# Output projection as seven block products in float16 parts, and a first value projection in plain float32

## The chip, the cores and the metric

The kernel runs on one core of a Trainium2 chip. Its time is the device time of that core in microseconds (us). The engines are named as in the profile: PE is TensorE with its matmuls, PEld its weight loads, DVE is VectorE, ACT is ScalarE, POOL is GpSimd, and SP is the engine whose queue issues nearly all DMAs. The program fixes the order of the instructions on each engine's queue.

## The reference, cut to what matters

One layer over 4096 frames of width 1024, all in float32:

```python
u = rms_norm(h, norm_g)                      # 4096 x 1024
p = u @ w_in                                 # 1024 x 4616: q, k, v, z of eight heads,
(sb_q, sb_k, sb_v, sb_z,                     #   q, k, v, o, z of four heads, two gates
 m_q, m_k, m_v, m_o, m_z, m_i, m_f) = split(p)
sb = stick_breaking_attention(sb_q, sb_k, sb_v) * silu(sb_z)
ml = head_layer_norm(mlstm_chunkwise(conv(m_q, m_k), m_v, m_i, m_f) * sigmoid(m_o)) * silu(m_z)
mix = concatenate([sb, ml])                  # 4096 x 1024
h = h + mix @ w_out                          # the output projection, 1024 x 1024
out = rms_norm(h, final_norm_g)
```

## The kernel before, in words

A frame tile is 128 frames; there are 32. A block is four tiles. The program makes four sweeps over the eight blocks: two for the stick-breaking heads (four heads each), two for the mLSTM heads (two heads each), and then the output projection, called stage C here. Normalised frames are transposed once, cut into a high and a low float16 part (`U`), stored to DRAM (`scr_u`, `u_store` L469) and read again by each sweep. Weights are scaled by a power found from their largest element (`Prep.top` L269, `Prep.scale` L282) and cut into float16 parts in the same way (`Prep.split` L293). A product of two cut operands takes three matmuls, high by high, high by low and low by high.

The order of the work is written out by hand. Time is counted in quanta: one quantum is the 24 matmuls of one weight group against one block (`t_quantum` L473), or the same amount of other matmuls. Helper steps are hung on a quantum with `at(g, phase, fn)` and issued by `run(g, phase)` ahead of its matmuls ("pre"), after half of them ("mid") or after its finishing step ("post"). Since the queues are in order, a helper step that makes PE wait holds all matmuls behind it.

**Start (L1180 to L1281).** SP loads frame tiles 0 and 1, the first value weights with the gate columns (four pieces of 256 KB and one of 32 KB), tiles 2 and 3, and the weight groups q0, k0; q1, k1, z0, z1 follow as buffers come free. Each weight group goes through `top` (DVE), a transpose on PE in `scale` (L284) with a short DVE chain after it, and `split` on POOL or DVE with ACT between. The value weights go through it first, and only then the value projections of tiles 0 to 2 run (`n_mm` L486, 264 columns, 24 float16 matmuls each; the fourth comes a little later through `sb_nat`). Then q1 and k1 are prepared, and the first quantum (q0) starts. In that quantum and the next, `z0.scale` and `z1.scale` are hung on "mid", between the two halves of the matmuls, and their `top` on "pre".

**Stage C (L1050 to L1178).** During the last block of the mLSTM the eight pieces of `w_out` are loaded and cut into two float32r parts (`wo_load` L1052, ACT and POOL). For each frame tile the mixed result is read from DRAM (`m_load` L1096), cut into two float32r parts (`m_split` L1110: ACT and DVE), and multiplied by the two halves of `w_out`: 24 matmuls of 512 columns for one half tile (`c_mm` L1119), accumulated in one PSUM bank. `c_add` (L1129) adds the residual on DVE and squares on ACT; `c_norm` (POOL) and `c_out` (DVE) normalise, and SP stores. The very last half tile is done in two pieces of 256 columns (`c_last` L1142). The last steps of the mLSTM's last block overlap the stage's first quanta.

The core of a product in stage C before:

```python
for k in range(KT):
    for j, (a, w) in enumerate(((0, wh), (1, wh), (0, wl))):
        PE.matmul(ps, u[:, a, k, :], w[:, cs], start=..., stop=...)
```

The functions that the change touches:

Of the kernel before, what the change touches and what calls it, by code (L numbers as in the profile page):

```python
# [9 lines left out]
F32 = mybir.dt.float32  # L10
# [10 lines left out]
DM = 1024  # L21
# [18 lines left out]
S_A = 2.0 ** 15  # L40


@with_exitstack
def hymba_kernel(ctx: ExitStack, tc: tile.TileContext, x, norm_g, w_in, b_ig, b_fg, conv_w,
# [9 lines left out]
    scr_m = dram.tile([NT, 128, KT, 128], F32, name="scr_m")  # L54
    scr_M = dram.tile([ML_H, SEQ], F32, name="scr_M")
# [6 lines left out]
              scr_u, scr_m, scr_M, scr_E, flag)  # L62
# [136 lines left out]
def main_pass(ctx, tc, x2, norm_g, win, win_k, b_ig, b_fg, conv_w, conv_b, hn_g, wout_k, fn_g,  # L199
              out2, scr_u, scr_m, scr_M, scr_E, flag):  # L200
# [6 lines left out]
    st = ctx.enter_context(tc.tile_pool(name="st", bufs=5))  # L207
# [27 lines left out]
    SX = const.tile([128, 2, 2, 3], F32, name="SX")  # L235
    idf = const.tile([128, 128], F32, name="idf")
# [10 lines left out]
    D1 = const.tile([128, 512], F32, name="D1")  # L247

# [271 lines left out]
    def sb_scales(s):  # L520

        for pair in range(2):
            q, k, z = (inv(WTS[s, f"{n}{pair}"]) for n in "qkz")
# [3 lines left out]
            V.tensor_scalar(out=SX[:, s, pair, 2:3], in0=z, scalar1=1.0 / (S_QKV * S_A), scalar2=inv(WNS[s]),  # L527
                            op0=ALU.mult, op1=ALU.mult)
# [416 lines left out]
    at(sb_g(NB) - 1, "post", lambda: sb_scales(1))  # L945
# [103 lines left out]
    WO = {}  # L1049
    gl = ml_g(2 * NB - 1)  # L1050

    def wo_load(i):  # L1052
        box = []

        def ld():
            r = stage()
            half, k0 = (1, 2 * i) if i < 4 else (0, 2 * i - 8)
            SP.dma_start(out=r.rearrange("p (k c) -> p k c", k=2), in_=wout_k[:, k0:k0 + 2, 512 * half:512 * half + 512])
            box.append(r)

        def sp():
            key = ("ba"[i // 4], i % 4)
            if i < 6:
                WO[key] = [wp.tile([128, DM], F32R, tag="wT", name="wT", bufs=T_SLOTS) for _ in range(2)]
            else:
                t = wp.tile([128, 2 * DM], F32R, tag="wna", name="wna", bufs=2)
                WO[key] = [t[:, 0:DM], t[:, DM:2 * DM]]
            split(*WO[key], box.pop(), G)
        return ld, sp

    for i in range(8):
        ld, sp = wo_load(i)
        gi = gl + (1 + i if i < 3 else 2 + i)
        at(gi, "pre", ld)
        at(gi + 1, "mid", sp)
    for i, gm in enumerate((gl + 2, gl + 3, c_g - 1, c_g)):
        at(gm, "pre", lambda i=i: m_load(i))
        at(gm + 2, "mid", lambda i=i: m_split(i))
# [39 lines left out]

    def c_mm(ps, i, half, c0, n, mid=None):  # L1119
        u = mb[i // 2][:, i % 2]  # L1120
        for k in range(KT):
            wh, wl = WO["ab"[half], k // 2]
            cs = slice((k % 2) * 512 + c0, (k % 2) * 512 + c0 + n)
            for j, (a, w) in enumerate(((0, wh), (1, wh), (0, wl))):
                PE.matmul(ps, u[:, a, k, :], w[:, cs], start=(k == 0 and j == 0), stop=(k == KT - 1 and j == 2))  # L1125
            if k == 3 and mid:
                mid()

    def c_add(ps, hsl, sq):  # L1129
        V.tensor_tensor(out=hsl, in0=ps, in1=hsl, op=ALU.add)  # L1130
        A.activation(out=ph_tile("kl0", list(hsl.shape)), in_=hsl, func=AF.Square, scale=DM ** -0.5, accum_out=sq)  # L1131
# [254 lines left out]
```

## Time and profile before

| | |
|---|---|
| median of three runs | 2305.04 us (2304.14 to 2309.72) |
| the profiled execution, its own time | 2303.64 us |
| span from its first to its last instruction | 2301.9 us |
| PE busy | 2211.8 us, 96% |
| DVE, ACT, POOL busy | 1319.9, 1007.7, 719.3 us |
| TensorE clock granted, mean | 0.986 of full speed |

The profiled execution lies 1.4 us under the median of the runs, and 1.7 us of its time lie outside the span. The page cuts the span into 40 slices of 57.5 us; a digit is the busy share in tenths:

```profile
PE   4699999999999999999999999999999999999998
DVE  6477777756666666755555555654544445433332
POOL 2277667754555556511111112200000013100000
PEclk7899999999999999999999999999999999999999
```

In the first two slices PE is busy for four and six tenths and its clock is granted only in part. From the third slice to the last PE is full, and stage C fills the last six.

### The profile page before, as it was taken

The numbers are of one execution on the slowest core, as the hardware profiler recorded it, in microseconds if no ns is written. First come the engines' busy times: TensorE is split into PE (matmuls) and PEld (weight loads), VectorE is DVE, ScalarE is ACT, GpSimd is POOL, SyncE is SP. The second block draws the span as 40 slices with busy tenths as digits, with TensorE's granted clock in tenths as the row PEclk, the third lists the DMA queues.
The fourth block names the chain that finished last, engine by engine and source line by source line (L and its number), as shares of the span: only waits on it lengthen the run. The fifth ranks groups of instructions, "written<-read, shape, count | busy, mean of one in ns | idle before, by whom it ended". The sixth has DMA issues, their size and how long they took to land.

```text
span 2301.9 us, 36279 instructions
## 1 busy us (share of the span) xinstructions
PE 2211.8 (96%) x13945; PEld 1526.6 (66%) x13945; DVE 1319.9 (57%) x2725; ACT 1007.7 (44%) x1806; POOL 719.3 (31%) x1134
## 2 busy tenths in 40 slices
PE   4699999999999999999999999999999999999998
PEld 3366566666666666567767665666667677888887
DVE  6477777756666666755555555654544445433332
ACT  3477667656666666533333333222333334222221
POOL 2277667754555556511111112200000013100000
PEclk7899999999999999999999999999999999999999
DMA  6244444411111122112222232221222224444442
GB/s 184 52 90 93 93 98 97 112 46 47 65 57 56 56 67 84 59 51 74 74 74 74 74 92 47 65 65 57 60 55 65 61 74 138 146 138 150 152 137 93
DMA packets 221917, 193.98 MB, mean 84 GB/s; under 512 B 108084, under 2 KB 177768, under 8 KB 221736
## 3 DMA queue, kind: packets, MB, share of 16 engines
q1 hardware_dynamic: 221720, 191.59, 29.4%
q8 instruction: 111, 1.82, 0.3%
q14 instruction: 70, 0.57, 0.1%
q10 hardware_dynamic: 16, 0.00, 0.0%
HBM read 141.09 MB, written 50.46 MB: 83 GB/s over the span
## 4 chain that ended last, share of the span: by engine, by line
PE 73%; DVE 6%; issue 1%; ACT 1%; DMA 0%; POOL 0%; POOLq 0%; DVEq 0%; ACTq 0%
PE ps_pj L480 31%; PE ps_pj L492 17%; PE ps_pj L1125 15%; PE ps_zu L823 1%; DVE z L778 1%; PE ps_at L617 1%; PE ps_o L633 1%; PE ps_zu L866 1%; PE ps_zu L867 1%; DVE c L738 1%; PE ps_at L824 1%; PE ps_o L848 1%; PE ps_zu L848 1%; PE ps_at L894 1%; PE ps_zu L586 1%
## 5 line engine op out<-in xcount | busy, mean ns | idle before, releaser
L480 PE MATMUL ps_pj<-U,wT 128*128 128x512 f16 x4608 | 1045.0, 382 | 0.0
L480 PEld LDWEIGHTS <-wT 128*128 128x128 f16 x4608 | 452.5, 99 | 494.4 <-issue 11.4
L492 PEld LDWEIGHTS <-U 128*128 128x128 f16 x4608 | 452.1, 98 | 82.8 <-DVE kl L565 11.9
L492 PE MATMUL ps_pj<-wna,U 128*128 128x256 f16 (+1 forms) x3072 | 361.7, 276 | 17.4 <-DVE kl L565 7.5
L1125 PE MATMUL ps_pj<-wT,U 128*128 128x512 f32 (+1 forms) x1164 | 267.8, 387 | 0.0
L1125 PEld LDWEIGHTS ps_pj<-wT,U 128*128 128x128 f32 x1164 | 216.6, 188 | 44.3
L601 POOL TENSOR_TENSOR sA<-sA,bP 128x510 f32<-128x510 f32 x128 | 151.7, 1185 | 199.2 <-DVE bP L600 180.4
L600 DVE TENSOR_TENSOR_SCAN bP<-bP,D 128x512 f32<-128x512 f32 x128 | 162.9, 1273 | 53.1 <-POOL bP L592 52.9
L492 PE MATMUL ps_pj<-wnb,U 128*128 128x256 f16 x1536 | 178.1, 273 | 0.0
L1131 ACT ACTIVATE kl<-st 128x512 f32<-128x512 f32 (+1 forms) x65 | 40.7, 625 | 274.1 <-DVE st L1130 265.8
L879 POOL TENSOR_SCALAR rs<-mv 128x4 f32<-128x4 f32 x32 | 8.0, 250 | 483.7 <-DVE kl L773 448.4
L774 ACT ACTIVATE kl<-ps_pj,SC 128x512 f32<-128x512 f32 x64 | 44.0, 687 | 242.0 <-PE ps_pj L480 208.9
L1130 DVE TENSOR_TENSOR st<-ps_pj,st 128x512 f32<-128x512 f32 (+1 forms) x65 | 44.4, 683 | 173.9 <-PE ps_pj L1125 170.7
L825 DVE TENSOR_TENSOR bP<-ps_zu,bP 128x512 f32<-128x512 f32 x32 | 22.1, 691 | 203.5 <-PE ps_at L824 202.4
L778 DVE SCALAR_TENSOR_TENSOR z<-kl,CT,z 128x512 f32<-128x512 f32 x144 | 118.3, 821 | 19.8 <-ACT z L775 15.2
L622 DVE SCALAR_TENSOR_TENSOR ATl<-ps_at,ATh 128x512 f16<-128x512 f32 (+1 forms) x128 | 87.8, 686 | 41.3 <-ACT ATh L621 39.2
L810 POOL TENSOR_SCALAR_AFFINE_SELECT bP<-bP 128x512 f32<-128x512 f32 x32 | 24.3, 760 | 270.0 <-DVE bP L809 239.8
L787 ACT ACTIVATE v<-ps_pj,SC 128x256 f32<-128x256 f32 x64 | 30.3, 474 | 168.8 <-PE ps_pj L492 168.2
L1170 POOL TENSOR_SCALAR ss<-hs 128x1 f32<-128x1 f32 x31 | 9.6, 311 | 292.3 <-ACT kl L1131 292.3
L563 ACT ACTIVATE kh<-ps_pj 64x512 f16<-64x512 f32 x128 | 75.6, 590 | 57.4 <-PE ps_pj L480 39.1
L1125 PE MATMUL ps_pj<-wna,U 128*128 128x512 f32 (+1 forms) x396 | 92.8, 383 | 0.0
L537 ACT ACTIVATE zml<-ps_pj,SC 128x512 f32<-128x512 f32 x32 | 22.0, 687 | 159.8 <-DMA scr_m<-zml 144.8
(233 smaller groups left out, 3458.8 us busy)
## 6 DMA issues: line engine op xcount, KB each, us to landing
U<-scr_u SPq DMA_DIRECT2D x96, 512.0 KB
st<-in_x_dram SPq DMA_DIRECT2D x40, 512.0 KB
scr_u<-U SPq DMA_DIRECT2D x32, 512.0 KB
out_dram<-st SPq DMA_DIRECT2D x31, 512.0 KB
st<-in_w_in_dram SPq DMA_DIRECT2D x28, 512.0 KB
z<-scr_m SPq DMA_DIRECT2D x56, 256.0 KB
st<-in_x_dram SPq DMA_DIRECT2D x96, 128.0 KB
scr_m<-z SPq DMA_DIRECT2D x32, 256.0 KB
```

The source lines that it names most:

```text
L480: PE.matmul(p3, wt[:, a, k, :], u[:, :, b, k, :], start=(k == 0 and i == 0), stop=(k == KT - 1 and i == 2))
L492: PE.matmul(ps[:, c0:c0 + n], u[:, a, k, :], w[:, b, k, 0:n], start=first and j == 0, stop=last and j == len(order) - 1)
L563: A.activation(out=kh[d, h, 128:640], in_=ps[e], func=AF.Copy, scale=S_QKV)
L600: V.tensor_tensor_scan(out=bf, data0=bf, data1=D1[:, ::-1], initial=1.0, op0=ALU.mult, op1=ALU.max)
L601: G.tensor_tensor(out=sg[:, :, 0:255], in0=sg[:, :, 0:255], in1=b[:, :, 1:256], op=ALU.mult)
L622: V.scalar_tensor_tensor(out=l[:, i:, :], in0=ps[:, i:, :], scalar=S_A, in1=h[:, i:, :], op0=ALU.mult, op1=ALU.subtract)
L774: A.activation(out=raw[:, 3:515], in_=ps, func=AF.Copy, scale=inv(sid))
L778: V.scalar_tensor_tensor(out=y, in0=raw[:, t:t + 512], scalar=CT[:, 8 * t + grp:8 * t + grp + 1], in1=y, op0=ALU.mult, op1=ALU.add)
L848: PE.matmul(ps[:, j, :], mK[hh][:, c, :], vaug(p0 + c, hh), start=True, stop=True)
L1125: PE.matmul(ps, u[:, a, k, :], w[:, cs], start=(k == 0 and j == 0), stop=(k == KT - 1 and j == 2))
L1130: V.tensor_tensor(out=hsl, in0=ps, in1=hsl, op=ALU.add)
L1131: A.activation(out=ph_tile("kl0", list(hsl.shape)), in_=hsl, func=AF.Square, scale=DM ** -0.5, accum_out=sq)
```

## The change

**Stage C.** Frame tiles are taken in pairs. The two tiles of a pair and the two halves of the 1024 inner columns make a 2 x 2 block matrix A (rows: tile 2p and 2p+1; columns: inner columns 0 to 511 and 512 to 1023); `w_out` makes a 2 x 2 block matrix B. A times B is formed by seven block products instead of eight, in Winograd's form of Strassen's scheme. With A and B scaled to a common largest value (`total_top`), the left operands are

```
o=0: a11   o=1: s1 = a21+a22   o=2: a12   o=3: s2 = s1-a11
o=4: s4 = a12-s2   o=5: s3 = a11-a21   o=6: a22
```

and the right ones are the like sums of B. Both sides are cut into float16 parts; a block product is 4 x 3 = 12 matmuls of 512 columns. Products 0, 3, 5, 6 accumulate in one PSUM bank, 1 and 4 in a second, 2 has a third. DVE reads a bank after each product and adds it, scaled back, to the residual (`c_add`), also between products that go on accumulating in it.

The right operands are built during the last mLSTM sweep (`wo_top`, `wo_build`): eight loads for the maxima, eight again for the sums, ACT scales, POOL forms the sums and the low parts, ACT the high parts; three of the seven go to DRAM (`scr_w`) and are read back when the buffers of the last block's weights come free (`tw_load`). The left operands of pair p are made by `m_load`, `m_top` (four DVE maxima), `m_bound` (a matmul against a tile of ones on PE, then a short DVE chain), `m_scale` (ACT), `m_combine` (four sums on POOL), `m_high` (ACT), `m_low` (three on DVE, four on POOL). They are hung on steps counted from the pair's first product t0:

```diff
-    def c_mm(ps, i, half, c0, n, mid=None):
-        u = mb[i // 2][:, i % 2]
-        for k in range(KT):
-            wh, wl = WO["ab"[half], k // 2]
...
+    def total_top(src, n, top, out_scale, out_back, back):
+        ps = ps_tile("zu", [128, 8])
+        PE.matmul(ps[:, 0:n], ones, src, start=True, stop=True)
+        mx = sm.tile([128, 1], F32, tag="wx", name="wx")
+        V.tensor_reduce(out=mx, in_=ps[:, 0:n], op=ALU.max, axis=AX.X)
+        V.tensor_scalar(out=mx, in0=mx, scalar1=1e-30, scalar2=1.0 / top, op0=ALU.max, op1=ALU.mult)
+        V.reciprocal(out=out_scale, in_=mx)
+        V.tensor_scalar(out=out_back, in0=mx, scalar1=back, scalar2=None, op0=ALU.mult)
...
+    def m_top(p):
+        un[p] = sm.tile([128, 6], F32, tag="mtop", name="mtop", bufs=4)
+        for i, t in enumerate(mt[p]):
+            V.tensor_reduce(out=un[p][:, i:i + 1], in_=t.rearrange("p k t -> p (k t)"), op=ALU.max, axis=AX.X,
+                            apply_absolute_value=True)
+
+    def m_bound(p):
+        u = un[p]
+        total_top(u[:, 0:4], 4, M_TOP, u[:, 4:5], u[:, 5:6], SO[:, 1:2])
+
+    def m_scale(p, js):
+        for j in js:
+            A.activation(out=mt[p][j], in_=mt[p][j], func=AF.Copy, scale=un[p][:, 4:5])
+
+    def m_combine(p):
+        a11, a12, a21, a22 = mt[p]
...
+        G.tensor_tensor(out=s1, in0=a21, in1=a22, op=ALU.add)
+        G.tensor_tensor(out=s2, in0=s1, in1=a11, op=ALU.subtract)
+        G.tensor_tensor(out=s4, in0=a12, in1=s2, op=ALU.subtract)
+        G.tensor_tensor(out=s3, in0=a11, in1=a21, op=ALU.subtract)
+        mt[p] = [a11, s1, a12, s2, s4, s3, a22]
...
+    def m_low(p, os):
+        for o in os:
+            (V if o in (0, 2, 6) else G).tensor_tensor(out=mo[p][:, o, 1], in0=mt[p][o], in1=mo[p][:, o, 0], op=ALU.subtract)
...
+    def c_product(p, o, ps, first, last):
+        a, (wh, wl) = mo[p][:, o], TW[o]
+        for k in range(4):
+            for i, (l, r) in enumerate(((0, wh), (1, wh), (0, wl))):
+                PE.matmul(ps, a[:, l, k, :], r[:, k, :], start=first and k == 0 and i == 0, stop=last and k == 3 and i == 2,
+                          skip_group_check=True)
+
+    def c_add(p, ps, i, half):
+        t = xt[2 * p + i][:, half * 512:(half + 1) * 512]
+        V.scalar_tensor_tensor(out=t, in0=ps, scalar=un[p][:, 5:6], in1=t, op0=ALU.mult, op1=ALU.add)
...
+    for p in range(NP):
+        seq += [(p, 0), (p - 1, 6)] if p else [(p, 0)]
+        seq += [(p, o) for o in ((1, 2, 3, 4, 5) if p < NP - 1 else (1, 3, 2, 5, 4, 6))]
...
+        atp(t0 - 13, lambda p=p: m_load(p))
+        atp(t0 - 9, lambda p=p: m_top(p))
+        atp(t0 - 8, lambda p=p: m_bound(p))
+        atp(t0 - 7, lambda p=p: m_scale(p, (2, 3)))
+        atp(t0 - 7, lambda p=p: m_scale(p, (0, 1)))
+        atp(t0 - 6, lambda p=p: m_combine(p))
+        atp(t0 - 5, lambda p=p: m_high(p, (0, 2, 6)))
+        atp(t0 - 4, lambda p=p: m_low(p, (0, 2, 6)))
+        atp(t0 - 4, lambda p=p: m_high(p, (1, 3)))
+        atp(t0 - 3, lambda p=p: m_low(p, (1, 3)))
+        atp(t0 - 3, lambda p=p: m_high(p, (4, 5)))
+        atp(t0 - 2, lambda p=p: m_low(p, (4, 5)))
```

Each step of `seq` is issued after what is hung on it. `c_norm` and `c_out` of a pair's first tile stand on the first two steps of the next pair, those of its second tile on the third and fourth. The last half tile is no longer cut in two.

**Start.** The value weights with the gates are loaded right behind frame tile 0 into one float32 tile `vraw`, multiplied by `norm_g` (first half DVE, second half POOL) and used as they are; the transposed frames are kept in float32 (`u32`) for this. `v_mm` makes one tile's value projection with eight float32 matmuls. The scale of the value weights is found later and only scales the result. The frames' float16 parts and their stores (`u_parts`) come after that, the preparation of q0 and k0 is moved ahead of them, q1 and k1 are prepared around the first quanta, and z0 and z1 later than before. The float16 parts of the value weights, which the next seven blocks need, are made on POOL and ACT in quanta 8 and 10.

```diff
+        def v_mm(p):
+            ps = vps[p] = ps_tile("pj", [128, 512])
+            for k in range(KT):
+                PE.matmul(ps[:, 0:264], u32[p][:, k, :], vraw[:, k, :], start=(k == 0), stop=(k == KT - 1))
...
-        u_first(0, lambda: u_scale(1))
-        pv.top()
-        pv.scale()
-        pv.split([G, V, G, V, V])
...
+        u_scale(1)
+        v_mm(0)
+        u_first(1)
+        v_top()
+        u_stats(2)
+        v_mm(1)
+        v_scale()
+        v_fin(0)
...
+        qk[0].split([G, V])
+        u_parts(0, V)
+        u_parts(1, V)
+        v_fin(2)
+        qk[1].top()
+        v_mm(3)
+        qk[1].scale()
+        qk[1].split([G, V])
+        u_parts(2, V)
+        v_fin(3)
+        u_parts(3, V)
...
+        qk[2].top()
+        at(2, "mid", qk[2].scale)
+        at(2, "mid", lambda: qk[2].split([G, V]))
+        at(2, "post", qk[3].top)
+        at(3, "mid", qk[3].scale)
...
+            at(3 + i, "post" if i == 0 else "pre", lambda box=box: box[0].top())
+            at(4 + i, "mid", lambda box=box: box[0].scale())
...
+        at(8, "mid", lambda: G.tensor_scalar(out=vs, in0=vs, scalar1=SC[:, WNS[0], 0:1], scalar2=None, op0=ALU.mult))
+        at(10, "pre", lambda: A.activation(out=pn[:, 0], in_=vraw, func=AF.Copy))
+        at(10, "post", lambda: G.tensor_tensor(out=pn[:, 1], in0=vraw, in1=pn[:, 0], op=ALU.subtract))
```

The pool of staging tiles grows from five to six.

## Rows read from the trace of the kernel before

**Rows 1.** Stretches: length, then busy time per engine, clock granted, DMA share, GB/s.
```profile
0.00:20.00 20.00, 8.02 (x40) 7.31 (x41) 10.29 (x27) 6.61 (x14) 6.26 (x16) 0.81 0.81 239
...
0.00:118.65 118.65, 71.95 (x359) 43.40 (x360) 65.19 (x161) 45.86 (x95) 34.75 (x52) 0.80 0.42 118
1938.40:2293.10 354.70, 354.70 (x1613) 294.86 (x1611) 138.85 (x239) 78.12 (x192) 35.09 (x69) 1.00 0.41 140
```

**Rows 2.** Timeline of PE in stage C: start, length, line, shape, count.
```profile
2260.00 8.32 PE L1125 MATMUL ps_pj<-wT,U 128*128 128x512 f32 x36
2268.16 2.88 PE L1125 MATMUL ps_pj<-wna,U 128*128 128x512 f32 x12
2270.88 8.32 PE L1125 MATMUL ps_pj<-wT,U 128*128 128x512 f32 x36
...
2290.07 1.60 PE L1125 MATMUL ps_pj<-wT,U 128*128 128x256 f32 x12
2291.51 1.60 PE L1125 MATMUL ps_pj<-wna,U 128*128 128x256 f32 x12
```

**Rows 3.** Timeline of PE in an mLSTM sweep: float16 quantum, then float32 matmuls.
```profile
1508.26 5.34 PE L480 MATMUL ps_pj<-U,wT 128*128 128x512 f16 x24
1513.44 0.61 PE L848 MATMUL ps_o<-v,ATh 128*128 128x130 f32 x4
1513.89 0.61 PE L848 MATMUL ps_zu<-v,ATh 128*128 128x130 f32 x4
```

**Rows 4.** Groups by line from 1900 us on: shapes, count, busy, mean ns, idle before.
```profile
L1130 DVE TENSOR_TENSOR st<-ps_pj,st 128x512 f32<-128x512 f32 x63 | 43.5, 691 | 171.1 <-PE ps_pj L1125 167.8 <-DMA st<-in_x_dram 3.3
L1131 ACT ACTIVATE kl<-st 128x512 f32<-128x512 f32 x63 | 39.8, 632 | 269.9 <-DVE st L1130 261.6 <-issue 8.2
L251 DVE TENSOR_TENSOR U<-z,U 128x512 fp32r<-128x512 f32 x56 | 36.2, 688 | 37.0 <-ACT U L250 37.0
L250 ACT ACTIVATE U<-z 128x512 fp32r<-128x512 f32 x56 | 31.9, 617 | 0.0
L1178 DVE SCALAR_TENSOR_TENSOR st<-st,ss,O 128x512 f32<-128x512 f32 x31 | 23.1, 746 | 0.0
...
L1171 POOL TENSOR_TENSOR ss<-ss,mhalf 128x1 f32<-128x1 f32 x31 | 17.7, 570 | 2.6
```

**Rows 5.** Timeline of DVE in the start: two maxima over 512 columns.
```profile
67.42 1.27 DVE L273 TENSOR_REDUCE wm<-ATh 128x4 f32<-128x512 f32 x2
```

**Rows 6.** Timeline of DVE and POOL: start, and first stick-breaking sweep.
```profile
16.13 1.54 POOL L301 TENSOR_TENSOR bP<-bP,wgs 128x512 f32<-128x512 f32 x1 [7.55 <-DVE wgs L291]
...
422.74 1.09 POOL L601 TENSOR_TENSOR sA<-sA,bP 128x510 f32<-128x510 f32 x1 [1.15 <-DVE bP L600]
...
423.94 2.13 POOL L378 TENSOR_TENSOR U<-st,U 128x1024 f16<-128x1024 f32 x1
...
427.49 1.27 POOL L691 TENSOR_TENSOR z<-z,O 128x512 f32<-128x512 f32 x1
...
431.05 1.20 DVE L378 TENSOR_TENSOR U<-st,U 128x1024 f16<-128x1024 f32 x1
431.27 1.92 POOL L601 TENSOR_TENSOR sA<-sA,bP 128x510 f32<-128x510 f32 x1 [1.69 <-DVE bP L600]
```

**Rows 7.** Timeline of PE in the start, with the idle time before and its releaser.
```profile
23.93 5.44 PE L492 MATMUL ps_pj<-wna,U 128*128 128x264 f16 x24 [7.16 <-ACT wna L296]
...
55.04 5.22 PE L480 MATMUL ps_pj<-U,wT 128*128 128x512 f16 x12
69.40 0.48 PE L284 MATMUL ps_zu<-idf,wmb 128*128 128x128 f32 x1 [9.13 <-DVE wmb L280]
...
84.91 0.48 PE L284 MATMUL ps_zu<-idf,wmb 128*128 128x128 f32 x1 [7.04 <-DVE wmb L280]
...
117.78 0.60 PE L617 MATMUL ps_at<-idf,sA 128*128 128x128 f32 x4
```

**Rows 8.** Timeline at the end: the last store's issue.
```profile
2296.08 0.90 SPq L1162 DMA_DIRECT2D out_dram<-st  x1
```

More of the change, by code (lines that the diff above doesn't have):

```diff
@@ L40 @@
 S_A = 2.0 ** 15
+M_TOP = 8192.0
 @with_exitstack
@@ L1056, in ld @@
             r = stage()
-            half, k0 = (1, 2 * i) if i < 4 else (0, 2 * i - 8)
-            SP.dma_start(out=r.rearrange("p (k c) -> p k c", k=2), in_=wout_k[:, k0:k0 + 2, 512 * half:512 * half + 512])
+            SP.dma_start(out=r, in_=wout_k[:, i, :])
             box.append(r)
[L1061 to L1064, printed above, removed]
-            else:
-                t = wp.tile([128, 2 * DM], F32R, tag="wna", name="wna", bufs=2)
-                WO[key] = [t[:, 0:DM], t[:, DM:2 * DM]]
-            split(*WO[key], box.pop(), G)
@@ L1080, in main_pass, with tw_load @@
+    for j in range(4):
+        wo_build(j, g3 + 20 + ML_SLOTS * j)
+    def tw_load(o):
+        t = [wp.tile([128, 4, 512], F16, tag="wT", name="wT", bufs=T_SLOTS) for _ in range(2)]
+        for i in range(2):
+            SP.dma_start(out=t[i], in_=scr_w[o - 4, :, i])
+        TW.append(t)
+    for o in (4, 5, 6):
+        at(gl + 2 * o - 5 if o < 6 else gl + 6, "pre", lambda o=o: tw_load(o))
     fng = [None, None]
@@ L1119, in c_mm @@
-    def c_mm(ps, i, half, c0, n, mid=None):
-        u = mb[i // 2][:, i % 2]
-        for k in range(KT):
-            wh, wl = WO["ab"[half], k // 2]
[L1123 to L1131, printed above, removed]
@@ new lines, in c_add, with c_square @@
+    def c_add(p, ps, i, half):
+        t = xt[2 * p + i][:, half * 512:(half + 1) * 512]
+        V.scalar_tensor_tensor(out=t, in0=ps, scalar=un[p][:, 5:6], in1=t, op0=ALU.mult, op1=ALU.add)
+    def c_square(p, i, half):
+        t = 2 * p + i
+        if t not in hs2:
+            hs2[t] = sm.tile([128, 2], F32, tag="hs2", name="hs2", bufs=4)
+        A.activation(out=ph_tile("kl0", [128, 512]), in_=xt[t][:, half * 512:(half + 1) * 512], func=AF.Square, scale=DM ** -0.5,
+                     accum_out=hs2[t][:, half:half + 1])
@@ new lines, in c_done, with c_step @@
+    def c_done(p, ps, i, half):
+        c_add(p, ps, i, half)
+        c_square(p, i, half)
+    def c_step(p, o):
+        if o == 0:
+            cps[p] = [ps_tile(tag, [128, 512]) for tag in ("pj", "o", "zu")]
+        b1, b2, b3 = cps[p]
+        if o == 0:
+            c_product(p, o, b1, True, False)
+            c_add(p, b1, 0, 0)
+        elif o == 1:
+            c_product(p, o, b2, True, False)
+            c_add(p, b2, 1, 1)
+        elif o == 2:
+            c_product(p, o, b3, True, True)
+            c_done(p, b3, 0, 0)
+        elif o == 3:
+            c_product(p, o, b1, False, False)
+            c_add(p, b1, 0, 1)
+        elif o == 4:
+            c_product(p, o, b2, False, True)
+            c_done(p, b2, 0, 1)
+        elif o == 5:
+            c_product(p, o, b1, False, False)
+            c_done(p, b1, 1, 1)
+        else:
+            c_product(p, o, b1, False, True)
+            c_done(p, b1, 1, 0)
@@ L1350, in main_pass @@
         at(c_g + 9, "mid", lambda: flag_max(accT, flag, 1))
[L1351 to L1354 removed]
+        for n, (p, o) in enumerate(seq):
+            run(c_g + n // 2, "mid" if n % 2 else "pre")
+            c_step(p, o)
+            if n % 2:
+                run(c_g + n // 2, "post")
+        for g in range(c_g + len(seq) // 2, c_g + len(seq) // 2 + 4):
             for phase in ("pre", "mid", "post"):
```

345 lines of the change are left out of this document (197 added, 148 removed).

## The prediction, made before the change was run

> **What bounds the kernel now.** I read the page's slices first, then the busy times of two stretches, the timelines of PE and the groups by line. In the slices PE is full from the third on, so there only PE's own work counts. In stage C it is busy for all of its 354.7 us [rows 1], with DVE at 39% and POOL at 10%: no product waits for an operand. The first 118.65 us are another matter: PE is busy for 72.0 us of them, at a mean clock of 0.80 [rows 1]. Its long waits there are for DVE, in the scale step L284: 9.13 us before 69.40 and 7.04 us before 84.91 [rows 7], both in the middle of a weight quantum. A microsecond of PE work removed from stage C is one gained; a microsecond saved in the start is gained if the chain of preparation gets shorter.
>
> **Stage C, the products.** 48 matmuls go from 2260.00 to 2270.88, 226.7 ns each, and 12 of 256 columns take 1.44 us [rows 2]. So 1512 x 0.2267 + 48 x 0.12 = 348.5 us; the other 6 us of the stretch are the mLSTM's last steps. After: 16 pairs x 7 x 12 = 1344 matmuls in float16 of the same 512 columns. 24 of these take 1513.44 - 1508.26 = 5.18 us, 215.8 ns each [rows 3], and a step of 12 takes 2.59 us. 1344 x 0.2158 = 290.0 us. Of the 58.5 us removed, 43.5 are the 192 matmuls and 15 the faster type. This much is gained if PE never waits.
>
> **The bound's matmul.** Sixteen `m_bound`s put a float32 matmul against a tile of ones into PE's queue. Four float32 pieces of 130 columns take 0.45 us, 112 ns each, and a float32 matmul is two pieces [rows 3]; with 4 columns the weight loads decide instead, and one takes 294.86 / 1611 = 0.18 us on average in stage C [rows 1]. I take 0.4 us (0.2 to 0.6): 6.4 us.
>
> **The wait in front of it.** This is what I think decides. `m_top`, four DVE maxima, stands one step ahead of `m_bound`, which PE meets a step later with all products queued behind it. Two maxima take 1.27 us [rows 5], so four take 2.54, nearly the step's 2.59; whatever DVE has left over from before is waited for by PE. At best DVE begins right behind the `c_add` of the product just ended: that product's result after 0.2, 0.69 for the add [rows 4], 2.54 for the maxima, less the 2.59 of the step: 0.9 us of wait.
>
> It begins later where DVE is held. Durations for one pair: `c_add` 0.69 like L1130, `c_out` 2 x 0.66 (the pitch of L1178's 0.75), a low part on DVE 0.65 to 0.69 like L251, ACT 0.6 each like L250 and 0.8 for a square with its sum like L1131, `c_norm` 0.9, of which L1171 is 0.57 and the rest a small operation ahead of it [rows 4]. POOL takes 1.27 for a plain product of 512 and 2.13 / 2 = 1.07 for a low part [rows 6]; I take 1.15 for all eight. What matters is that the two engines stop each other: L601 on POOL takes 1.09 us alone, but 1.92 us when a DVE operation with two SBUF inputs (1.20 us from 431.05) runs over its first 0.98 us [rows 6], so it loses 0.83 of them.
>
> The Trainium skill says this too (GPSIMD Engine Reference, section Specifications): the SBUF interfaces are shared, with contention for DVE instructions that have two SBUF inputs. By it `c_out` and the DVE low parts are held, while `c_add` and the maxima are not; without it the second rival below is the sum.
>
> I stepped the queues through one pair, in us from its first product. ACT scales the next pair's pieces until 4.1. POOL's four sums begin at 2.9, are held 1.3 by the first tile's `c_out`, and end at 8.9; `c_norm` of the second tile stands behind them, ends at 9.7, and POOL then takes a low part until 10.9. DVE's queue has stood at that tile's `c_out` all the while. It starts at 10.9, does `c_out` and three low parts until 14.2, two `c_add`s until 15.5, and the maxima until 18.1. PE has ended six products at 15.5: it waits 2.6 us. I take 2.6 for each of 14 pairs in the stage: 36.4 us. The lower bound is the 0.9 above; the upper 4.5, which the same walk gives with POOL at the 1.54 that L301 shows beside DVE [rows 6]. Banks cost nothing: `c_add` of product 3 ends at 15.5, product 5 begins behind the bound at 18.5.
>
> **The other ends of stage C.** Pairs 0 and 1 are prepared while the mLSTM's last block still needs DVE, and 2 MB of products and 3 MB of operands are loaded in the same five quanta: 4 us (2 to 8). At the end the last half tile is whole. Today the last store is issued 2296.08 - 2293.10 = 3.0 us behind PE [rows 1, 8]; after, the add, the square, `c_norm` and two `c_out`s make 0.2 + 0.69 + 0.8 + 0.9 + 1.4 and some 0.2 of hand-overs, 4.2 us: 1.2 more.
>
> **Building the right operands.** Sixteen loads of 512 KB, 44 POOL operations (some 51 us), 36 on ACT and 8 maxima are spread over the last mLSTM sweep, and the eight old splits disappear. PE is full there and POOL nearly idle in the page's slices; what is hidden stays hidden as long as POOL does not hold up DVE's convolution steps. I take 2 us (0 to 8). The value weights' parts on POOL in quanta 8 and 10 are two operations of 2112 columns, 4 to 5 us each at 1.07 to 1.27 per 512 [rows 6]; the attention steps queue behind them in a slice with POOL at seven tenths, and have a quantum and a half to spare: 1 us (0 to 4).
>
> **The start.** The value projection begins at 23.93 today, after its weights were scaled and split [rows 7]. It could begin at about 14 after: the weights land at 8 to 9 (1.5 MB with tile 0, at the mean of 239 GB/s over the first 20 us [rows 1], from 0.8 on, and the landing), DVE takes 1.3 for its half and POOL, held by it, ends its half at 14. But each tile now costs 16 float32 pieces of 264 columns, 0.112 x 264 / 130 = 0.228 each [rows 3], 3.6 us at full clock and up to 7.3 at half, against 24 in 5.44 at half clock [rows 7]. The frames' parts are made after the projections (1.05 on ACT and 1.25 on DVE per tile), with q0 and k0 ahead of them; SP takes their four stores later, which nobody waits for until the second sweep. Stepping the queues, the last part is ready at 54 and the first quantum starts there: 55.04 today [rows 7], so nothing is won up to that point. What is won comes after: the waits of 9.13 and 7.04 for z0 and z1 go, and 2.1 for k1 and 4.9 for z0 remain in my walk, 9.2 less. Behind such a wait the first half quantum runs at half clock, 5.22 instead of 2.59 [rows 7]; there are three such halves now and two after: 2.8 less. 12 us (4 to 18).
>
> **The sum.** -58.5 + 6.4 + 36.4 + 4 + 1.2 + 2 + 1 - 12 = -19.5 us. From the profiled execution's 2303.64 that is 2284.1; its time lies 1.4 under the median, so 2285.5, say 2285.
>
> **The rivals.**
> *DVE is not held.* If the adds and low parts on POOL and DVE hardly meet, the wait is 0.9 a pair: 14 x 1.7 = 24 us less, 2262. For it: rows 6 show the loss for two tensor inputs only, none for the three-operand form of `c_out`. Against it: the norm of the second tile stands behind 4.6 us of POOL work whether or not the port is shared.
> *POOL holds the stage.* With POOL operations at 1.54 the walk waits 4.5 us a pair, 14 x 1.9 = 27 more: 2312, slower than before. The change turns slower from a wait of 2.6 + 19.5 / 14 = 4.0 us. For it: L301 at 1.54 beside DVE [rows 6]. Against it: that row's DVE operation, an own 0.7 long, is in the walk already, so taking 1.54 for all counts it twice.
> *The start wins nothing.* If the float32 projections run at half clock throughout and the preparation is no shorter, 12 us more: 2297.5. For it: DVE's queue sets the pace there, and its work doesn't shrink. Against it: the four q and k maxima no longer stand behind two quanta's operations.
>
> **How the numbers follow.** Forecast 0.48 (its own range 2270 to 2298), DVE not held 0.25, start wins nothing 0.15, POOL holds the stage 0.12. A measurement of this kernel tells about 0.3%, 6.9 us, from no change. Faster by more: 0.46 + 0.25 + half of 0.15, 0.78. Within: the other half of 0.15, some of the forecast's upper end and of the POOL case's lower end, 0.15. Slower: 0.07. The range reaches from the middle of the first rival's spread to the break-even: 2252 to 2304.
>
> **What would show it.** In stage C after: 12 float16 matmuls in 2.59 us; a wait of PE on the DVE maxima at the matmul against ones, once a pair, 2.6 us long (0.9 if DVE is not held); a pair lasting 21.1 us (19.4; 23 if POOL holds). DVE idle for POOL ahead of the second tile's `c_out`. In the start: the first quantum near 54, the first stick-breaking block's last weight matmul some 12 us before 117.8. The prediction is wrong if PE's wait sits elsewhere (on a bank, on a load), if the clock falls in stage C because of the waits, or if the last mLSTM sweep lengthens by more than 8 us.

## The result, and the profile after

The changed kernel takes 2340.05 us (median of 4 runs, 2338.94 to 2342.00) against 2305.36 before (the median of 4): a ratio of 1.0146, 95% interval 1.0133 to 1.0158. It is slower by 1.5%; the forecast was 2285. Its profiled execution, the slowest of the four, has a span of 2340.2 us against 2301.9, 38.3 more. Where they lie is read from the first weight matmul of each block (line 480 before, 486 after) and the first and last product of stage C. Blocks are counted from 0 through all four sweeps, so that block 24 is the first of the last sweep:

| stretch | before | after | difference | forecast |
|---|---|---|---|---|
| start to block 1 | 118.65 | 110.57 | -8.1 | -12 |
| block 1 to block 24 | 1326.9 | 1338.4 | +11.5 | +1 |
| block 24 to the first product of stage C | 492.8 | 518.8 | +26.0 | +2 |
| stage C, first to last product | 354.7 | 362.4 | +7.7 | -11.7 |
| last product to the end | 8.8 | 10.0 | +1.2 | +1.2 |

**Stage C.** The same two stretches as in [rows 1], with the same columns (length, busy time and instructions of PE, of its weight loads, DVE, ACT and POOL, granted clock, DMA share, GB/s), after:

```profile
0.00:110.57 110.57, 77.05 (x328) 46.58 (x329) 67.41 (x152) 44.84 (x90) 33.65 (x50) 0.83 0.46 130
1967.79:2330.20 362.41, 319.90 (x1424) 144.34 (x1421) 248.06 (x379) 133.31 (x289) 189.72 (x183) 0.95 0.38 129
```

In the second line PE is no longer busy throughout: 42.5 us idle, and the clock is 0.95 where it was 1.00. The waits of PE over the whole run (us in total, times, the longest) name who ends the idle time. Of the second row five waits, 19.2 us, lie in the last sweep; the longest, 5.6, lies ahead of it and stands in the kernel before too. The timeline of two pairs (start, length, line, count, idle time before and its releaser) shows what follows it:

```profile
PE ps_zu L1066 <- DVE mtop L1204: 41.1, 15, 3.2
PE ps_at L904 <- DVE zml L906: 24.9, 6, 5.6
```

```profile
2105.04 0.39 PE L1066 MATMUL ps_zu<-mtop,ones 128*128 128x4 f32 x2 [3.00 <-DVE mtop L1204]
2105.28 7.93 PE L1245 MATMUL ps_pj<-wT,U 128*128 128x512 f16 x36
2113.05 2.75 PE L1245 MATMUL ps_o<-wT,U 128*128 128x512 f16 x12
...
2126.68 0.38 PE L1066 MATMUL ps_zu<-mtop,ones 128*128 128x4 f32 x2 [3.12 <-DVE mtop L1204]
2126.93 9.62 PE L1245 MATMUL ps_pj<-wT,U 128*128 128x512 f16 x36
...
2150.04 0.39 PE L1066 MATMUL ps_zu<-mtop,ones 128*128 128x4 f32 x2 [3.13 <-DVE mtop L1204]
```

A step of 12 takes 2115.64 - 2113.05 = 2.59 us, as forecast. The wait in front of the bound is 3.0 to 3.1 us, not 2.6. Behind the second one 36 matmuls take 9.62 us instead of 7.93: the granted clock falls to its lower level, 1.2 of 2.4 GHz. The trace has 11 such stretches of 3.4 us in stage C, ten behind a bound and one behind a wait for a bank, each costing half its length: 18.8 us. Pairs without one last 21.64 us (2105.04 to 2126.68), with one 23.36 (2126.68 to 2150.04). The stretch adds up: 1344 x 0.2158 = 290.0 of products, 14 x 0.24 = 3.4 for the bounds that lie in it (2105.04 to 2105.28 for one), 42.5 idle, 18.8 at the low clock, and the 6.2 of the mLSTM's last steps that the stretch had before too (354.7 - 348.5): 360.9 of 362.4.

The groups by line in stage C after (count, busy time and mean ns, idle time before), to be held against [rows 4]:

```profile
L1237 POOL TENSOR_TENSOR U<-sA,U 128x512 f16<-128x512 f32 x56 | 75.3, 1365 | 56.9 <-ACT U L1233 56.9
L1301 DVE SCALAR_TENSOR_TENSOR st<-st,ss,c 128x512 f32<-128x512 f32 x30 | 48.0, 1600 | 0.0
L1250 DVE SCALAR_TENSOR_TENSOR st<-ps_pj,mtop,st 128x512 f32<-128x512 f32 x64 | 47.5, 744 | 74.9 <-PE ps_pj L1245 74.9
...
L1301 DVE SCALAR_TENSOR_TENSOR st<-st,ss,yx 128x512 f32<-128x512 f32 x30 | 31.2, 1042 | 16.6 <-POOL ss L1294 16.6
...
L1237 DVE TENSOR_TENSOR U<-v,U 128x512 f16<-128x512 f32 x21 | 19.9, 998 | 0.0
...
L1204 DVE TENSOR_REDUCE mtop<-z 128x1 f32<-128x512 f32 x28 | 17.1, 669 | 0.0
```

`c_out` has the form of L1178 in [rows 4], 746 ns there with POOL at 10% [rows 1]; beside POOL's sums and low parts its two halves take 1042 and 1600 on average. DVE's low parts take 998 on average instead of 688: where one runs beside a POOL operation it takes 1.64 us, elsewhere 0.68. What reads one operand from PSUM (L1250, at most 753 ns) and the maxima (L1204, at most 675) take no longer beside POOL than without it. DVE's queue in the pair above, from the second tile's `c_out` to the maxima:

```profile
2117.86 0.75 DVE L1301 SCALAR_TENSOR_TENSOR st<-st,ss,yx 128x512 f32<-128x512 f32 x1 [1.27 <-POOL ss L1294]
...
2118.53 1.64 DVE L1301 SCALAR_TENSOR_TENSOR st<-st,ss,c 128x512 f32<-128x512 f32 x1
2120.10 2.84 DVE L1237 TENSOR_TENSOR U<-v,U 128x512 f16<-128x512 f32 x3
...
2122.86 0.74 DVE L1250 SCALAR_TENSOR_TENSOR st<-ps_zu,mtop,st 128x512 f32<-128x512 f32 x1
...
2124.18 2.45 DVE L1204 TENSOR_REDUCE mtop<-z 128x1 f32<-128x512 f32 x4
```

It stands idle for the norm, runs without a gap from there, and ends the maxima at 2126.63: PE's wait ends at 2126.68.

**The last mLSTM sweep.** Each of the four blocks with a build takes 66.4 to 66.7 us instead of 60.9. First two rows of before, PE's wait for the gating in block 24 and DVE's four scalings in block 27; then DVE, POOL and PE after, in block 27:

```profile
1478.07 0.66 PE L894 MATMUL ps_at<-idf,ATl 128*128 128x128 f32 x4 [1.40 <-DVE zml L896]
...
1647.22 1.11 DVE L886 TENSOR_SCALAR ATl<-ATl,mv,rs 128x128 f32<-128x128 f32 x4
```

```profile
1668.62 1.59 POOL L1117 TENSOR_TENSOR st<-st 128x512 f32<-128x512 f32 x1
1669.01 4.85 DVE L896 TENSOR_SCALAR ATl<-ATl,mv,rs 128x128 f32<-128x128 f32 x4
...
1672.63 2.26 POOL L1142 TENSOR_TENSOR wT<-st,wT 128x512 f16<-128x512 f32 x2
1673.79 1.13 DVE L783 COPY kl<-halo 128x3 f32<-128x3 f32 x1
...
1678.97 0.66 PE L904 MATMUL ps_at<-idf,ATl 128*128 128x128 f32 x4 [3.91 <-DVE zml L906]
1679.47 4.08 PE L486 MATMUL ps_pj<-U,wT 128*128 128x512 f16 x11
```

POOL's operations run back to back, and DVE's four scalings of 128 columns take 4.85 us instead of 1.11, one behind each of POOL's; even a copy of three columns takes 1.13. The gating L906 comes late, PE waits 3.91 for it, and a low-clock stretch of 3.4 us begins (11 matmuls in 4.08): 3.9 + 1.7 = 5.6 us a build. The four builds make 22.7 of the 26.0 us, block 24 makes 4.9, and the last block, 31, is 1.7 shorter. There the trace of the kernel before already has this picture, beside three operations of the old splits on POOL (1896.60 to 1904.96):

```profile
1899.85 5.19 DVE L886 TENSOR_SCALAR ATl<-ATl,mv,rs 128x128 f32<-128x128 f32 x4
...
1908.34 0.66 PE L894 MATMUL ps_at<-idf,ATl 128*128 128x128 f32 x4 [3.52 <-DVE zml L896]
```

**The start.** PE, after, against [rows 7]:

```profile
11.03 5.98 PE L1398 MATMUL ps_pj<-vraw,wT 128*128 128x264 f32 x16 [1.09 <-DVE vraw L1430]
...
49.54 0.58 PE L486 MATMUL ps_pj<-U,wT 128*128 128x512 f16 x1 [6.09 <-ACT U L1389]
...
64.50 0.33 PE L290 MATMUL ps_zu<-idf,wmb 128*128 128x128 f32 x1 [2.43 <-DVE wmb L286]
...
75.83 0.33 PE L290 MATMUL ps_zu<-idf,wmb 128*128 128x128 f32 x1 [3.26 <-DVE wmb L286]
75.99 4.44 PE L486 MATMUL ps_pj<-U,wT 128*128 128x512 f16 x12
...
87.46 0.33 PE L290 MATMUL ps_zu<-idf,wmb 128*128 128x128 f32 x1 [3.13 <-ACT sA L600]
...
97.62 0.32 PE L1365 MATMUL ps_zu<-idf,O 40*128 40x40 f32 x1 [3.35 <-ACT sA L600]
...
109.69 0.60 PE L627 MATMUL ps_at<-idf,sA 128*128 128x128 f32 x4
```

The lead at block 1 is gone at block 2 (172.07 before, 171.50 after). All three engines there:

```profile
117.23 5.68 POOL L1487 TENSOR_SCALAR vraw<-vraw,SC 128x2112 f32<-128x2112 f32 x1
...
136.51 5.66 DVE L455 TENSOR_SCALAR zml<-st,r 128x256 f32<-128x256 f32 x4
...
136.95 4.24 POOL L1489 TENSOR_TENSOR wna<-vraw,wna 128x2112 f16<-128x2112 f32 x1
...
143.35 0.27 PE L440 MATMUL ps_zu<-sq,gs 128*128 128x8 f32 x1 [2.76 <-POOL sq L436]
```

### The profile page after: what moved, and what is told of

Its sections match the earlier page's. It is cut to its first block, busy times and chain, and to the rows that moved or that the text cites. A ratio compares the mean times of both kernels' runs of the same rounds, so it can differ in the third digit from the quotient of the medians.

```text
span 2340.2 us, 36288 instructions
## 1 busy us (share of the span) xinstructions
PE 2198.8 (94%) x13731; PEld 1385.2 (59%) x13731; DVE 1484.4 (63%) x2885; ACT 1087.1 (46%) x1939; POOL 939.7 (40%) x1297
## 4 chain that ended last, share of the span: by engine, by line
PE 57%; DVE 14%; issue 4%; POOL 4%; ACT 2%; DMA 0%; SPq 0%; POOLq 0%; DVEq 0%; ACTq 0%
PE ps_pj L486 29%; PE ps_pj L498 16%; DVE U L1237 2%; DVE z L788 2%; PE ps_pj L1245 2%; DVE st L1301 1%; DVE mtop L1204 1%; PE ps_at L627 1%; PE ps_o L643 1%; PE ps_zu L833 1%; DVE ATl L896 1%; PE ps_zu L876 1%; PE ps_zu L877 1%; DVE st L1250 1%; POOL sA L1224 1%
## 5 line engine op out<-in xcount | busy, mean ns | idle before, releaser
L498 PEld LDWEIGHTS <-U 128*128 128x128 f16 x4512 | 442.5, 98 | 71.7 <-DVE kl L575 10.2
L498 PE MATMUL ps_pj<-wna,U 128*128 128x256 f16 (+1 forms) x2976 | 349.0, 275 | 9.0 <-DVE kl L575 6.3
L1245 PEld LDWEIGHTS <-U 128*128 128x128 f16 x1344 | 136.0, 102 | 169.9 <-issue 26.2
L1245 PE MATMUL ps_pj<-wT,U 128*128 128x512 f16 x576 | 145.1, 416 | 2.4 <-DVE st L1250 2.4
L1256 ACT ACTIVATE kl<-st 128x512 f32<-128x512 f32 x64 | 40.3, 630 | 230.2 <-issue 136.8
L1237 POOL TENSOR_TENSOR U<-sA,U 128x512 f16<-128x512 f32 x56 | 75.3, 1365 | 56.9 <-ACT U L1233 56.9
L1250 DVE SCALAR_TENSOR_TENSOR st<-ps_pj,mtop,st 128x512 f32<-128x512 f32 x64 | 47.5, 744 | 74.9 <-PE ps_pj L1245 74.9
L600 ACT ACTIVATE sA<-ps_zu,SX 128x512 f32<-128x512 f32 x128 | 88.4, 691 | 0.0
```

What stands on the lines that cost most here:

```text
L498: PE.matmul(ps[:, c0:c0 + n], u[:, a, k, :], w[:, b, k, 0:n], start=first and j == 0, stop=last and j == len(order) - 1)
L600: A.activation(out=sg, in_=z, func=AF.Sigmoid, scale=SX[:, s, pair, 0:1])
L1237: (V if o in (0, 2, 6) else G).tensor_tensor(out=mo[p][:, o, 1], in0=mt[p][o], in1=mo[p][:, o, 0], op=ALU.subtract)
L1245: PE.matmul(ps, a[:, l, k, :], r[:, k, :], start=first and k == 0 and i == 0, stop=last and k == 3 and i == 2, skip_group_check=True)
L1250: V.scalar_tensor_tensor(out=t, in0=ps, scalar=un[p][:, 5:6], in1=t, op0=ALU.mult, op1=ALU.add)
```

## The experiments

All are edits of the kernel after unless the text says otherwise, with one execution each but for the last two. The kernel before took 2306.66 beside `c_bound_later`, `c_fill`, `wo_shift` and `vraw_act`, and 2307.43 beside `pool_only`, `c_out_step`, `c_both` and `all_four`.

**The bound one step later** (`c_bound_later`).
```diff
-        atp(t0 - 8, lambda p=p: m_bound(p))
+        atp(t0 - 7, lambda p=p: m_bound(p))
```


> m_bound is hung one step (12 matmuls) later, two steps behind m_top instead of one; nothing else differs from the changed kernel. Theory A (stage C is lengthened by PE's wait for the maxima at the bound's matmul, 3.0 to 3.2 us a pair, and by the half clock that follows most of the waits, 1.7 us each): the wait goes to 0.5 us or less, no half clock in the steady part, a pair takes 18.4 to 19 us instead of 22.5, and the time falls by 50 to 57 us, from 2340 to 2283 to 2290. Rival B (VectorE and GpSimd bound the stage, the wait would only move to a bank or to the operands): a pair stays at 21 us or more and the time falls by 20 us at most.

Measured: 2292.61, 47 less. The waits of PE in stage C, and a pair:

```profile
PE ps_pj L1245 <- DVE st L1250: 15.1, 15, 2.7
```

```profile
2122.91 2.75 PE L1245 MATMUL ps_pj<-wT,U 128*128 128x512 f16 x12 [0.82 <-DVE st L1250]
...
2125.64 5.34 PE L1245 MATMUL ps_pj<-wT,U 128*128 128x512 f16 x24
```

Past the first pairs the wait on the maxima and the low clock are gone (one low-clock stretch is left, behind a wait of 2.73 for a bank); a pair takes 19.25 us. It misses theory A's band by 3 us, since a wait of 0.8 to 0.9 for a PSUM bank took its place: the `c_add` that frees the bank is late in DVE's queue.

**Work instead of idleness** (`c_fill`): 14 matmuls whose result nobody reads, ahead of the bounds.
```diff
     def m_bound(p):
         u = un[p]
+        if 3 <= p:
+            f = ps_tile("at", [128, 512])
+            for i in range(14):
+                PE.matmul(f, mo[p - 2][:, 5, 0, i % 4, :], TW[0][0][:, i % 4, :], start=True, stop=True)
         total_top(u[:, 0:4], 4, M_TOP, u[:, 4:5], u[:, 5:6], SO[:, 1:2])
```


> As the changed kernel, but from pair 3 on 14 more float16 matmuls of 512 columns, whose result nobody reads, stand in PE's queue ahead of each bound's matmul, so that PE works through what was the wait (14 x 0.216 = 3.0 us). If the idle time itself makes the clock fall (theory A), the granted clock stays at full in the steady part, the idle time at the bound is 0.2 us or less and the stage gains the half-clock time, about 1.25 us a pair on average: 2340 falls by 13 to 18 us, to 2322 to 2327, although PE does 182 matmuls more. If the clock falls for another reason, the half-clock stretches stay, and the time is 2340 or more.

Measured: 2325.67. From the fourth on, a pair takes 21.65 to 21.83, the period of the undisturbed pairs, and no low-clock stretch is left behind a bound:

```profile
2094.89 3.19 PE L1212 MATMUL ps_at<-wT,U 128*128 128x512 f16 x14
2098.17 0.39 PE L1066 MATMUL ps_zu<-mtop,ones 128*128 128x4 f32 x2
2098.41 7.93 PE L1249 MATMUL ps_pj<-wT,U 128*128 128x512 f16 x36
```

3 us more matmuls in each of 13 pairs made the kernel 14 us faster: in these pairs the clock fell because PE stood still.

**The builds four quanta later** (`wo_shift`).
```diff
-        wo_build(j, g3 + 20 + ML_SLOTS * j)
+        wo_build(j, g3 + 24 + ML_SLOTS * j)
```


> As the changed kernel, but the four builds of the right operands in the last mLSTM sweep start four quanta later, so that GpSimd's sums and low parts fall into the quanta of the value projections, when VectorE has little to do, and not into those of the convolution and the layer norm. Theory A (GpSimd operations in a row hold VectorE's short two-port operations there, and TensorE waits for the transposes' bank behind them, with half clock after it, 5.6 us a build): the four blocks that took 66.5 us go back to 61 to 62, the time falls by 18 to 24 us, to 2316 to 2322. Rival B (it is the amount of GpSimd and ScalarE work, or the DMA traffic, in the sweep): the blocks stay at 65 us or more, the time within 6 us of 2340.

Measured: 2313.98, a little below the band. Blocks 26 to 30 take 60.93 each, as before the change, and PE waits nowhere on L906 from 1500 to 1900 us: the same work costs nothing in another part of the block. The span is 27.9 us shorter than that of the profiled execution of the kernel after: 22.7 of them are the four blocks', 1.2 block 24's, and 3.3 came ahead of it, which the edit does not touch.

**GpSimd's share of the build alone** (`pool_only`), an edit of the kernel before.
```diff
...
+    def jsum(n):
+        for _ in range(n):
+            G.tensor_tensor(out=jf, in0=D1, in1=D1, op=ALU.subtract)
+    def jlow(n):
+        for _ in range(n):
+            G.tensor_tensor(out=jh, in0=D1, in1=jf, op=ALU.subtract)
+    for j in range(4):
+        g = ml_g(NB) + 20 + ML_SLOTS * j
+        at(g + 3, "pre", lambda: jsum(2))
+        at(g + 3, "post", lambda: jsum(2))
+        for i, n in enumerate((2, 2, 2, 1)):
+            at(g + 4 + i, "post", lambda n=n: jlow(n))
```


> The kernel before, with GpSimd's share of the building of the right operands and nothing else of the change: in each of the last sweep's blocks with a build, 4 sums and 7 subtractions of 128x512 in SBUF at the same places, on tiles that nobody else uses; no loads, no ScalarE work, no weights (the values are dropped). Theory A (GpSimd's two-input operations alone hold DVE's short operations, DVE comes late, the transposes of the normalised heads wait and the next steps run at half clock): each of the four blocks takes 66 to 67 us instead of 60.9, the whole 2326 to 2332 against 2306.7. Rival B (ScalarE's 9 operations a build, the DMA traffic or the staging buffers): the blocks stay at 60.9 and the time within 2304 to 2309.

Measured: 2337.10, 30 more than before. The four blocks take 66.2 to 68.2 us, 26.8 more in all, with the same picture:

```profile
1663.59 5.15 POOL L1056 TENSOR_TENSOR jf<-D 128x512 f32<-128x512 f32 x4
1665.54 4.63 DVE L888 TENSOR_SCALAR ATl<-ATl,mv,rs 128x128 f32<-128x128 f32 x4
...
1676.16 1.11 PE L896 MATMUL ps_at<-idf,ATl 128*128 128x128 f32 x4 [4.34 <-DVE zml L898]
```

No load, no ScalarE operation and no staging buffer is in it, so rival B falls. It goes past A's band by 5: 3 us went between blocks 4 and 8, where this kernel is the one before, and PE's wait is 4.3 instead of 3.9 in three of the four blocks: the low parts, which wait for nothing here, stand closer together (four in 6.07 us right behind the sums).

**The value weights off GpSimd** (`vraw_act`).
```diff
-        at(8, "mid", lambda: G.tensor_scalar(out=vs, in0=vs, scalar1=SC[:, WNS[0], 0:1], scalar2=None, op0=ALU.mult))
+        at(8, "mid", lambda: A.activation(out=vs, in_=vs, func=AF.Copy, scale=SC[:, WNS[0], 0:1]))
...
-        at(10, "post", lambda: G.tensor_tensor(out=pn[:, 1], in0=vraw, in1=pn[:, 0], op=ALU.subtract))
+        at(10, "post", lambda: V.tensor_tensor(out=pn[:, 1], in0=vraw, in1=pn[:, 0], op=ALU.subtract))
```


> As the changed kernel, but the two operations of 2112 columns on the value weights in quanta 8 and 10 are moved from GpSimd: the scaling to ScalarE, the low part to VectorE. Theory A (GpSimd standing still for 5.7 and 4.2 us there held the attention steps, and that is where the 8.1 us that the start had won went): the second block takes 54 us as before instead of 61, the lead of 8 us over the kernel before is kept at the end of the first sweep (now it is 2.7 us behind there), the time falls by 7 to 11 us. Rival B (the first sweep is paced by VectorE and GpSimd anyway, so that any lead is given back): at the end of the first sweep the lead is 2 us or less whatever the second block does, the time falls by 0 to 4 us.

Measured: 2332.01, inside theory A's band. Block 1, which holds both operations, takes 56.21 us instead of 60.93, where it was 53.42 before the change: 4.7 of the 7.5 us lost there come back. What else is gained lies where the edit does not reach: block 0 is 2.0 us shorter and blocks 4 to 8 are 2.9, and both vary as much among kernels that are alike there (block 0 takes 58.9 to 61.0 us in the runs here, blocks 4 to 8 take 219.2 to 224.2). So the time came out as theory A has it in part by luck. At the end of the first sweep the lead over the kernel before is 6.9 us here, but 1.3, 8.4 and 2.4 in the three later kernels with the same edit (`all_four`, `all_four_timed`, `all_five`): whether the lead lasts is not shown.

**`c_out` of the second tile a step later** (`c_out_step`; with the later bound, `c_both`).
```diff
-        atp(n + 1, lambda p=p: c_out(2 * p + 1))
+        atp(n + (2 if p < NP - 1 else 1), lambda p=p: c_out(2 * p + 1))
```


> The changed kernel with c_out of each pair's second tile one step later (its norm unchanged). Theory A (DVE comes late to the maxima because its queue stands idle, 17.5 us in all, in front of that c_out until GpSimd has finished the sums and the norm): DVE uses the time for the low parts, the wait in front of the bound falls by about 1.2 us a pair, from 3.0 to 1.9, the half clock goes in most pairs, and the time is 2340 - 18 - 19 = 2303 (2297 to 2312). Rival B (the sum of DVE's work and its slowing by GpSimd set the time, the order does not matter): the wait stays at 3 us, 2336 to 2342.

> The changed kernel with both: m_bound one step later (measured alone at 2292.6, pairs of 19.25 us with a wait of 0.82 for a bank) and c_out of the second tile one step later. Theory A: the bank waits only because DVE, held at that c_out, comes late to the adds; a pair takes 7 x 2.59 + 0.25 = 18.4 us, the time is 2292.6 - 15 x 0.85 = 2280 (2277 to 2284). Rival B (DVE's work beside GpSimd's simply fills the pair): 19.2 a pair and 2290 to 2294.

Measured: 2311.50 and 2276.44. The waits of PE in stage C, for the one and the other:

```profile
PE ps_zu L1066 <- DVE mtop L1204: 23.7, 15, 1.8
```

```profile
PE ps_pj L1245 <- DVE st L1250: 2.7, 2, 1.8
```

In `c_out_step` the wait in front of the bound is at most 1.8, no pair past the first two is at the low clock, and a pair takes 20.25, as theory A has it; the time is near the band's upper end, with the stage 33 us shorter and not 37, and 2.4 us more ahead of it than in the run of after. In `c_both`, half a microsecond under A's band, a pair takes 18.27 us, 7 x 2.59 + 0.14: past the first pairs PE never waits, with POOL and DVE doing the same work as after. The order in the two queues was the whole loss of the stage, which lasts 300.8 us here.

**All of it** (`all_four`, timed again as `all_four_timed`; `all_five` has the output weights' maxima elsewhere).
```diff
+    WTOP = (1, 4, 5, 6, 7, 8, 9, 10)
...
-        at(g3 + 2 * i, "pre", ld)
-        at(g3 + 2 * i + 1, "mid", lambda: V.tensor_reduce(...
+        at(g3 + WTOP[i] - 1, "pre", ld)
+        at(g3 + WTOP[i], "mid", lambda: V.tensor_reduce(...
```
`all_four` has the two moves of `c_both` and the edits of `wo_shift` and `vraw_act`; the diff shows what `all_five` adds to them.

> c_both with the builds four quanta later and the value weights' scale on ScalarE, their low parts on DVE. If the losses are separate, they add up: 2280 - 26.1 - 8.0 = 2246 (2240 to 2252), faster than the kernel before by 60. If one of them only moves into another place (the builds then collide with the pairs' preparation, the start's lead is spent at a later block), 2255 or more.

> The kernel with all four moves, once more and timed: 2250 (2247 to 2253) against 2305 to 2307 before, a ratio of 0.975 to 0.977.

> The same with the eight maxima of the output weights in the first block of the last sweep in steps 1, 4, 5, 6, 7, 8, 9 and 10 of it instead of 1, 3, 5, ..., 15. Theory A: what that block loses (3.4 to 4.9 us in every run of the changed kernel) is the maximum of 1.2 us that stands in DVE's queue directly ahead of the convolution and the gating for which the transposes wait (3.62 us where it was 1.40, and a half-clock stretch behind it); with that maximum gone from there the block takes 62.7 us as before, the whole 2246 (2244 to 2248). Rival B (the loads, or the maxima wherever they stand): 2249 to 2252.

Measured: `all_four` 2250.05; timed, beside the kernel before at 2309.68, `all_four_timed` 2247.16 (ratio 0.9736, interval 0.9720 to 0.9752; the ratio is under the 0.975 expected because the kernel before took 2309.68 and not 2305 to 2307) and `all_five` 2248.69 (0.9743, 0.9727 to 0.9760). So a version with the change's own arithmetic beats the kernel before by 2.6%. The losses were separate: each had its own place, and the time of all four lies in the band that their sum gives. PE's second transposes in block 24, in `all_four_timed` and `all_five`:

```profile
1471.83 1.12 PE L904 MATMUL ps_at<-idf,ATl 128*128 128x128 f32 x4 [3.64 <-DVE zml L906]
```

```profile
1475.24 0.66 PE L904 MATMUL ps_at<-idf,ATl 128*128 128x128 f32 x4 [2.50 <-DVE zml L906]
```

The wait was 3.61 to 3.64 us in all nine other kernels with the change, and 1.40 before it. So the maximum ahead of the gating makes 1.1 of the 2.2 us by which the wait had grown; the other half stays open. The block shrinks from 66.4 to 63.8 us (62.7 before) and not to 62.7, as theory A has it, and only the wait's share of that is the edit's for certain: with the old place the block took 64.9 to 67.6, since the low clock followed the same wait in seven of the nine kernels and not in `c_bound_later` and `vraw_act`. In the time of the whole nothing is to be told: 2248.69 lies between the bands of the two theories, `all_five` was 3.5 us later in blocks 4 to 8, for no reason that its edit has, and the two intervals overlap.

## Why the prediction was wrong, step by step

The forecast was a gain of 19.5 us on the span, and the span grew by 38.3. The 57.8 us between are three terms.

*Building the right operands, +2 (0 to 8): measured +26.0, 24 too little.* This is the step that failed worst, and in its reason. "What is hidden stays hidden as long as POOL does not hold up DVE's convolution steps" named the condition and did not check it. I counted POOL's idle share of the sweep and not how much slack DVE has where the work falls; before the change PE already waited 1.40 us for the gating at one such place. The last block of the kernel before even had the whole price, beside the old splits: 5.19 us for the four scalings and a wait of 3.52. `pool_only` gives the loss with POOL alone, `wo_shift` takes it away with the place alone. 4.9 us are block 24's (2.2 to 4.9 over the runs); `all_five` puts half of its longer wait down to the maxima, and the rest is open.

*Stage C, -11.7: measured +7.7, 19.4 too little.* The products (290.0), their step (2.59) and the mLSTM's part were right, the bound's matmul smaller (0.24 for 0.4). The wait's mechanism and place were right, and its size was off by 0.5: in the walk the second tile's `c_out` and the low parts end 14.2 us behind the pair's first product (the second step behind the bound, 2105.28 + 2.59), in the trace 2122.86 - 2107.87 = 15.0. That it came so near is in part luck, since two errors offset each other: `c_out` begins at 10.0 and not at 10.9, but then it and the three low parts take 5.0 us and not 3.3, its second half and the first of them 1.64 each beside POOL's low parts. What was missing is the clock. I charged a wait at its own length; behind 11 waits PE ran at the low level, 18.8 us in all, nearly the whole difference. The prediction names that as something that would make it wrong, but gives it no price, though [rows 7] show a half quantum of 5.22 behind a long wait. `c_fill` shows it: same period, no idleness, no low clock.

The Trainium skill's rule was half read. The same sentence (GPSIMD Engine Reference, section Specifications) names, beside DVE instructions with two SBUF inputs, those in a 2-port performance mode, and the page "SBUF — State Buffer", section "SBUF: two separate sides", has the pair of ports as a lock that one operation holds for its whole length. The trace agrees: it is the one-input scalings (4.85 us for 1.11) and copies (1.13 for 0.14) that waited a whole POOL operation each, and these I had counted as free. That they ran in such a mode is not to be seen in a trace. What has two SBUF inputs was held too, `c_out`'s form among it (1.64 us for 0.75), which settles the doubt in the first rival; it is that rival, "DVE is not held", whose sum would hold without the rule, and not the second, as the prediction's sentence has it.

*The start and the value weights' parts, -12 and +1: measured +3.4 at block 24, 14.4 too little.* The projection began earlier than I said (11.03 for 14) and the first quantum too (49.54 for 54). But the waits of 9.13 and 7.04 gave way to four of 2.43 to 3.35, 12.2 us together where the walk left 7.0, two of them for ACT and not for DVE; behind three of the four a half quantum took 4.2 to 4.9 us. So the start won 8.1 at block 1 and not 12. Then the value weights' parts, +1 (0 to 4), cost 7.5 (`vraw_act`: 4.7 of it back, the rest is open): one scaling of 2112 columns on POOL took 5.68 us, longer than I took it (4 to 5), and DVE's scalings of the frames stood behind the other (5.66 for four, 2.44 in the quantum before). Another 2.2 went in block 2, of which 1.9 came back in block 3, and some 3 in blocks 4 to 8; the latter come and go in runs of any of these kernels.

*Right:* the tail (+1.2), the first pairs' extra cost (25.28 + 25.53 us for the first fourteen products, less the mLSTM's 6.2 and two bare pairs of 18.38: 7.8, for 4 with a range of 2 to 8, but with a wait at a bound and two low-clock stretches in it, which were not its reason), and the choice against the first rival: POOL and DVE do hold each other. "POOL holds the stage" (a wait from 4.0 on) did not happen; the stage turned slower at 3.1 because the clock adds to it.

## What to carry to other kernels

An idle engine is not free room: before work goes onto GpSimd, ask what VectorE does in the same microseconds, which of its operations stand behind a whole GpSimd operation, and who waits for them. A wait of TensorE is priced with the clock behind it: in stage C waits of 2.9 us and more mostly cost 1.7 us on top here, those below 2 us nothing but for one of 1.81. Where a small reduction stands between two stretches of matmuls, give it a step more than it needs, and look then for the next one in the queue (here a PSUM bank); moving three steps in time and two operations to other engines turned 1.5% slower into 2.6% faster.

## What the runs showed of the hardware that was not expected

- A VectorE copy of 128x3 elements took 0.14 us, and 1.13 us beside GpSimd's two-input operations; four of 128x128 took 1.11 and 4.85. Reductions from SBUF (669 ns for 512 columns) and operations with a PSUM operand (744 ns) took no longer beside them.
- In stage C the matmuls behind waits of TensorE of 0.8 to 1.96 us ran at full clock, but for one wait of 1.81 in `c_out_step`; behind one of 2.73 in `c_bound_later` 12 of them took 4.44 us; of the 13 waits of 2.9 to 3.2 in the kernel after, ten were followed by 3.4 us at 1.2 GHz.
- GpSimd's scaling of 128x2112 float32 by one value a partition took 5.68 us, its two-input subtraction of the same columns 4.24.
